# Loads and row squares of a streaming encoder layer: an early function table, third-group weight blocks in more places, squares tied behind another tile

## The chip, the cores and the metric

The kernel runs on one core of one Trainium2 chip. The metric is device time in microseconds of one execution. Before the change the median of three runs is 2246.33 us (2240.46 to 2246.46). One more execution was recorded by the hardware profiler; its own time is 2244.01 us.

Engines are named as in the profile: PE multiplies matrices (PEld loads its weights), DVE and ACT work on vectors, POOL is the general-purpose engine, SP issues most DMAs. Each engine runs its own instructions in order and waits on semaphores for the others.

## The reference

One layer over 2048 prompt rows and 64 rows of a running stream, all float32, width 1024. Only what the change touches is shown; what follows (output projection, squared-ReLU MLP of width 4096, final norm) is left out.

```python
def _rmsnorm(x, gain):
    y = xf * lax.rsqrt(jnp.mean(xf * xf, axis=-1, keepdims=True) + EPS)
    return (y * gain).astype(x.dtype)
...
a  = _rmsnorm(hp, norm1[l])
z  = a @ w_in                       # columns: qa, ka, va | qr, kr, vr, gr
qa, ka, qr, kr = rotated by position
attn_o = _swa_prompt(qa, ka, va, sinks[l])     # window of three 64-row chunks
ret_o, s_p = _retention_prompt(qr, kr, vr)     # decayed state per head
r = ret_o * lax.rsqrt(mean(ret_o * ret_o) + EPS) * silu(gr)
hp = hp + concat([attn_o, r]) @ w_out
hp = hp + _sqrelu_mlp(_rmsnorm(hp, norm2[l]), w_up, w_down)
```

The first norm's factor per row, rsqrt(mean(x²)+EPS), is not multiplied into x. It is applied to the projection's result, so it is first needed when a row tile's projection is rotated.

## The kernel before

The program has four stages: projection with attention and retention (to about 720 us), output projection, MLP up, MLP down. Every float32 product is made of three products of rounded parts: an operand is split into a high part (ACT copies it to the float32r type) and a low part (DVE or POOL subtracts); PE multiplies high·high, high·low and low·high (lines 548, 549, 551).

The first stage runs in two phases (`ph`), each with half of the heads. In a phase the weight columns stand in three groups `ci` = 0, 1, 2 (384, 512, 512 columns), each of eight blocks of 128 rows. `load_w` (113) brings a block into a raw buffer, `weights` (129) splits it: `split_scaled` writes the high part on ACT (86) and the low part on DVE (87). The rows of x come in 17 tiles: sixteen of 128 prompt rows (0 to 15) and one of 64 stream rows, tile 16, called S here. A tile passes through `group` (535) once per column group: 24 products on PE (16 for S, whose two parts share the array). Phase 0 begins with the pair (S, 0): groups (S,0), (0,0), (S,1), (0,1), (S,2), (0,2), written here as (tile, group); then come tiles 1 to 13 one by one, and the pair (14, 15).

After a tile's groups come its attention steps (`att_a` to `att_e`) and retention steps (`ret_a` to `ret_e`). `att_a` scales and rotates the first group (234, and 203 to 206: three DVE products and one POOL add into `zr`), `ret_a` rotates the second into `qk`, `ret_v` takes the third: two scaled copies (356) and the tanh of the gate (361). The transposes for attention (254, 217, 218) go to PSUM; ACT copies them into `qT` (256) and `kw` (222), which the scores `s` (286, 287) need. The transposes of `qk` go to `ptr` (369).

`load_aux` (164) brings a tile's rows by token into `xk` (one buffer) and its rotation table into `rt` (two buffers). In phase 0 it also makes the row factors: ACT squares `xk` and sums (172), then five short POOL instructions make `rs`, `hrs`, `ss` and `rsv` (174 to 179). `load_x` (143) brings the tile's transposed rows into `xr` (one buffer); ACT copies the high part (160), POOL subtracts the low part (161).

What sets the order: PE and SP follow the order in which the code is written (`manual_schedule`, 572); when a step of attention or retention comes due between PE's products is decided by a table of costs and delays (496, 497). ACT, DVE and POOL are ordered by a scheduler that estimates times. SP waits in order: a load into a buffer that is not free holds back all loads behind it, and it keeps eight DMAs under way. Loads on SP and copies that prepare later weights (625, DRAM to DRAM, with additions issued by POOL at 622) use the same DMA engines.

Buffers that matter here: `raw` has three (116), so the fourth block of a group loaded that way waits until the first is split. `wraw` (115) uses eight places of the pool `qp`, which hold the split blocks of other groups later. `ph` and `pl` (320, 321) are two buffers each, first used by `att_d`.

```python
    ws[0, 1] = weights(0, 1, [load_w(0, 1, k, True) for k in range(NK)])
    ...
    ws[0, 2] = weights(0, 2)
```

## Time and profile before

| | |
|---|---|
| median of 3 runs | 2246.33 us |
| profiled execution, its own time | 2244.01 us |
| its span (first to last instruction) | 2242.2 us |
| PE busy | 2210.4 us (99%) |
| DVE, ACT, POOL busy | 1468.0, 1117.6, 441.5 us |
| clock granted to PE, mean over the span | 0.992 of full |
| DMA moved | 515.91 MB, mean 230 GB/s |

How to read it: PE is busy nearly throughout, so time can leave the run only where PE stands still or runs at the lower of its two clocks (1.2 instead of 2.4 GHz). The list of waits names both, by the instruction that waited and the one that ended the wait; windows of the span give busy time and granted clock of each stretch. Ends of matrix products are modelled in the profile, so a distance between two starts is surer than a duration.

### The profile page before, as it was taken

How to read it: one execution, taken by the hardware profiler on the slowest of the kernel's cores; microseconds unless marked ns; L12 is line 12 of the kernel's file. 1: busy time of each engine (PE TensorE's matmuls, PEld its weight loads, DVE VectorE, ACT ScalarE, POOL GpSimd, SP SyncE). 2: the span in 40 equal slices, each digit the busy share in tenths (PEclk: the TensorE clock that was granted, in tenths of full speed). 3: DMA queues.
4: the chain of work that ended last, by engine and by line, in shares of the span. 5: the costliest groups of instructions: out<-in, count | busy, mean ns of one | idle time of the engine just before them, and what ended most of it. 6: DMA issues, size and time to landing. Idle time of an engine off the chain costs nothing.

```text
span 2242.2 us, 35648 instructions
## 1 busy us (share of the span) xinstructions
PE 2210.4 (99%) x13274; PEld 2114.8 (94%) x13274; DVE 1468.0 (65%) x2461; ACT 1117.6 (50%) x1982; POOL 441.5 (20%) x547
## 2 busy tenths in 40 slices
PE   8999999999999999999999999999999999999998
PEld 6888878888888899999999999999999999999998
DVE  5565446555556567787688668667666876677664
ACT  5454445444434443456565657556554444554452
POOL 4544443444433222200000000000001100120011
PEclk9999999999999999999999999999999999999999
DMA  6557864588644689579699769776976787677662
GB/s 193 162 170 188 224 175 143 145 206 216 159 107 122 208 289 337 186 265 361 229 319 353 268 230 323 235 233 210 367 259 228 266 288 240 229 277 268 236 209 80
DMA packets 240877, 515.91 MB, mean 230 GB/s; under 512 B 20144, under 2 KB 126320, under 8 KB 236608
## 3 DMA queue, kind: packets, MB, share of 16 engines
q1 hardware_dynamic: 231616, 469.62, 61.7%
q0 software_dynamic: 8512, 43.29, 9.3%
q8 instruction: 104, 1.70, 0.3%
q10 hardware_dynamic: 576, 0.72, 0.1%
q14 instruction: 69, 0.57, 0.1%
HBM read 411.19 MB, written 169.54 MB: 259 GB/s over the span
## 4 chain that ended last, share of the span: by engine, by line
PE 93%; DMA 3%; DVE 1%; POOL 1%; ACT 1%; issue 1%; SPq 0%; DVEq 0%; POOLq 0%; ACTq 0%
PE y L1073 10%; PE y L1074 9%; PE y L1072 9%; PE z L548 7%; PE z L549 7%; PE z L551 6%; PE b L901 4%; PE b L902 4%; PE b L900 4%; PE y L763 3%; PE y L765 3%; PE y L764 3%; PE a L901 3%; PE c L901 3%; PE a L902 3%; PE c L902 3%
## 5 line engine op out<-in xcount | busy, mean ns | idle before, releaser
L1073 PE MATMUL y<-vl,wd 128*128 128x352 f32 x1344 | 436.4, 325 | 0.0
L1074 PE MATMUL y<-vh,wd 128*128 128x352 f32 x1344 | 434.7, 323 | 0.0
L1072 PE MATMUL y<-vh,wd 128*128 128x352 f32 x1344 | 433.0, 322 | 0.0
L548 PE MATMUL z<-w,xh 128*128 128x512 f32 (+1 forms) x816 | 327.2, 401 | 0.7 <-DVE xh L161 0.6
L549 PE MATMUL z<-w,xh 128*128 128x512 f32 (+1 forms) x816 | 310.5, 380 | 4.8 <-DVE w L87 4.8
L1022 POOL TENSOR_TENSOR acc<-acc,sq 128x352 f32<-128x352 f32 x41 | 70.2, 1712 | 1216.5 <-ACT sq L1018 1216.5
L484 ACT ACTIVATE wd<-dr 128x1024 fp32r<-128x1024 f32 x168 | 177.4, 1056 | 252.6 <-PE y L1074 171.8
L484 ACT ACTIVATE wu<-upr 128x512 fp32r<-128x512 f32 x336 | 209.4, 627 | 179.3 <-PE b L902 88.8
L551 PE MATMUL z<-w,xl 128*128 128x512 f32 (+1 forms) x768 | 289.5, 377 | 0.1
L485 DVE TENSOR_TENSOR wu<-upr,wu 128x512 fp32r<-128x512 f32 x336 | 231.0, 693 | 71.0 <-ACT wu L484 56.4
L485 DVE TENSOR_TENSOR wd<-dr,wd 128x1024 fp32r<-128x1024 f32 x168 | 209.2, 1247 | 102.1 <-ACT wd L484 96.8
L1072 PEld LDWEIGHTS y<-vh,wd 128*128 128x128 f32 x1344 | 253.9, 189 | 0.0
L1074 PEld LDWEIGHTS y<-vh,wd 128*128 128x128 f32 x1344 | 252.4, 188 | 0.0
L1073 PEld LDWEIGHTS y<-vl,wd 128*128 128x128 f32 x1344 | 252.0, 188 | 0.0
L901 PE MATMUL b<-al,wu 128*128 128x352 f32 x576 | 185.8, 323 | 0.0
L900 PE MATMUL b<-ah,wu 128*128 128x352 f32 x576 | 185.6, 322 | 0.0
L902 PE MATMUL b<-ah,wu 128*128 128x352 f32 x576 | 185.4, 323 | 0.0
L549 PEld LDWEIGHTS z<-w,xh 128*128 128x128 f32 x816 | 156.8, 192 | 26.3 <-DVE w L87 8.3
L548 PEld LDWEIGHTS z<-w,xh 128*128 128x128 f32 x816 | 156.5, 192 | 19.7 <-DVE xh L161 0.8
L551 PEld LDWEIGHTS z<-w,xl 128*128 128x128 f32 x768 | 145.1, 189 | 23.8 <-DVE xl L161 0.4
L485 DVE TENSOR_TENSOR vl<-rv,vh 128x1408 fp32r<-128x1408 f32 x84 | 138.1, 1647 | 38.8 <-ACT vh L484 38.4
L484 ACT ACTIVATE vh<-rv 128x1408 fp32r<-128x1408 f32 x84 | 116.0, 1380 | 59.8 <-DMA rv<-vscr 42.2
(286 smaller groups left out, 4737.7 us busy)
## 6 DMA issues: line engine op xcount, KB each, us to landing
rv<-vscr SPq DMA_DIRECT2D x84, 704.0 KB, 5.4
vscr<-C SPq DMA_DIRECT2D x48, 1056.0 KB, 5.7
upr<-uscr SPq DMA_DIRECT2D x192, 256.0 KB, 4.7
dr<-sscr SPq DMA_DIRECT2D x96, 512.0 KB, 4.6
upr<-in_wup SPq DMA_DIRECT2D x144, 256.0 KB, 3.6
dr<-in_wdn SPq DMA_DIRECT2D x72, 512.0 KB, 5.2
uscr<-in_wup POOLq DMA_DIRECT2D x16, 1024.0 KB, 10.2
sscr<-in_wdn POOLq DMA_DIRECT2D x16, 1024.0 KB, 9.3
```

Source lines behind the costliest of these rows:

```text
L484: nc.scalar.activation(h, x, AF.Copy)
L485: nc.vector.tensor_sub(l, x, h.bitcast(F32))
L548: nc.tensor.matmul(z[:, :n], xh[:, k], wh, start=k == 0, stop=False)
L549: nc.tensor.matmul(z[:, :n], xh[:, k], wl, start=False, stop=k == NK - 1 and xl is None)
L551: nc.tensor.matmul(z[:, :n], xl[:, k], wh, start=False, stop=k == NK - 1)
L900: nc.tensor.matmul(o, wh, ah[:, k], start=k == 0 and i in (1, 6, 5), stop=False, skip_group_check=True)
L901: nc.tensor.matmul(o, wh, al[:, k], start=False, stop=False, skip_group_check=True)
L902: nc.tensor.matmul(o, wl, ah[:, k], start=False, stop=k == 3 and i in (2, 4, 3), skip_group_check=True)
L1022: nc.gpsimd.tensor_add(self.acc, self.acc, sq)
L1072: nc.tensor.matmul(o, wh, vh, start=f == 0, stop=False)
L1073: nc.tensor.matmul(o, wh, vl, start=False, stop=False)
L1074: nc.tensor.matmul(o, wl, vh, start=False, stop=f == 15)
```

## The change

Three things are changed.

1. A tiny ACT copy (`first`) stands at the start. ACT loads its function table in front of its first activation; the table load was part of the first weight block's split, which waits for that block's DMA.
2. The loads at the start are put in another order. Of column group 1, four blocks are loaded ahead of S's `xk` and `rt` instead of behind them. Of group 2, three blocks go to `raw`, four to the `ph` and `pl` buffers and all seven are issued ahead of the cache, state and aux loads; the eighth goes to `raw` behind the aux load of tile 0.
3. The square of a tile's rows with its POOL steps becomes a function of its own, `token_norm`. It is called later than the load: for the two first tiles at the start, else at the beginning of the tile's own first group (or of the group 0 of the tile before, where the load has been issued by then), and it is tied (`issue_after`) behind the last tanh (361, `ret_v`) or the last high-part copy of `att_a` (239) that was written before it.

```diff
+    first = cp.tile([128, 3], F32, name="first")
+    nc.scalar.activation(first, mhalf, AF.Copy)
...
-    def load_w(ph, c, k, spare=False):
+    def load_w(ph, c, k, spare=False, tag=None):
...
+            wk.tile([128, 512], F32, name="waraw", tag=tag, bufs=2) if tag else \
...
             nc.sync.dma_start(xk[:T], xtok[t0:t0 + T])
+            squares[t] = xk
         nc.sync.dma_start(rt[:T], rot[t0:t0 + T])
-        if ph == 0:
+        return rt
+
+    squares = {}
+    last_act = [None]
+
+    def token_norm(t):
+        t0, T = tok(t)
+        xk = squares.pop(t)
+        with tc.issue_after(last_act[0].ins) if last_act[0] is not None else ExitStack():
             nc.scalar.activation(xk[:T], xk[:T], AF.Square, accum_out=ss[:T, t:t + 1])
...
-        nc.scalar.activation(hl[:T, 768:832], zr[:T, 5], AF.Copy)
+        last_act[0] = nc.scalar.activation(hl[:T, 768:832], zr[:T, 5], AF.Copy)
...
-        nc.scalar.activation(sig[:T], gz, AF.Tanh, scale=hrs[:T, t:t + 1])
+        last_act[0] = nc.scalar.activation(sig[:T], gz, AF.Tanh, scale=hrs[:T, t:t + 1])
...
-    nc.sync.dma_start(rd, rdec)
...
+    raws = [load_w(0, 1, k, True) for k in range(4)]
+    nc.sync.dma_start(rd, rdec)
     xs[a] = [*x0, load_aux(*a)]
-    ws[0, 1] = weights(0, 1, [load_w(0, 1, k, True) for k in range(NK)])
+    raws += [load_w(0, 1, k, True) for k in range(4, NK)]
+    ws[0, 1] = weights(0, 1, raws)
+    token_norm(a[1])
+
+    raws = [load_w(0, 2, k, tag=(None, None, None, "ph", "ph", "pl", "pl")[k]) for k in range(NK - 1)]
     caches[0] = load_cache(0)
+    xs[b] = [*x1, load_aux(*b)]
+    token_norm(b[1])
+    raws.append(load_w(0, 2, NK - 1))
     load_states(0)
-    xs[b] = [*x1, load_aux(*b)]
     nc.sync.dma_start(sk, sinks)
     nc.gpsimd.tensor_scalar(nsk, sk, -1.0, None, op0=ALU.mult)
-    ws[0, 2] = weights(0, 2)
+    ws[0, 2] = weights(0, 2, raws)
...
+        for u in [u for u in squares if (0, u) in tiles[:n_ + 2] and ci == 0 or (0, u) == tiles[n_]]:
+            token_norm(u)
```

The change moves instructions in three places. SP at the start, behind the last block of group 1 (`raw` and `waraw` are blocks of group 2, `cf` the cache, `xk` and `rt` of tile 0; the numbers are those of the buffers). Before:

```order
L117 DMA wraw_211<-in_w1 128x512
L431 DMA cf_237<-in_cv 128x64
L432 DMA cf_237<-in_ck 128x64
L455 DMA sts0_240<-in_sret 128x128
L455 DMA sts1_242<-in_sret 128x128
L169 DMA xk_245<-in_xtok 128x1024
L170 DMA rt_244<-in_rot 128x384
L601 DMA sk_77<-in_sinks 128x8
L117 DMA raw_257<-in_w1 128x512
L117 DMA raw_262<-in_w1 128x512
L117 DMA raw_267<-in_w1 128x512
L117 DMA raw_272<-in_w1 128x512
```

The same place now:

```order
L120 DMA raw_239<-in_w1 128x512
L120 DMA raw_241<-in_w1 128x512
L120 DMA raw_243<-in_w1 128x512
L120 DMA waraw_245<-in_w1 128x512
L120 DMA waraw_247<-in_w1 128x512
L120 DMA waraw_249<-in_w1 128x512
L120 DMA waraw_251<-in_w1 128x512
L442 DMA cf_253<-in_cv 128x64
L443 DMA cf_253<-in_ck 128x64
L172 DMA xk_257<-in_xtok 128x1024
L174 DMA rt_256<-in_rot 128x384
L120 DMA raw_267<-in_w1 128x512
```

Seven blocks of group 2 moved ahead of seven other loads; one stands behind `xk` and `rt`.

POOL at the start, from the add that makes `zr` of tile S to the adds that make `qk` of S and of tile 0; `ms`, `rs`, `ss`, `hrs`, `rsv` are row factors of tile 0, the `cf` loads belong to phase 1. Before:

```order
L206 TENSOR_TENSOR zr<-rot_327,rot_328 64x320
L245 DMA out<-zr 64x64
L602 TENSOR_SCALAR nsk<-sk 128x8
L174 TENSOR_SCALAR ms<-ss 128x1
L431 DMA cf<-in_cv 128x64
L432 DMA cf<-in_ck 128x64
L175 TENSOR_TENSOR rs<-ms,mhalf 128x1
L177 TENSOR_SCALAR ss<-ms 128x1
L176 TENSOR_SCALAR hrs<-rs 128x1
L178 TENSOR_SCALAR rsv<-rd,rs 128x4
L206 TENSOR_TENSOR zr<-rot_391,rot_392 128x320
L206 TENSOR_TENSOR qk<-rot_423,rot_424 64x512
```

Now:

```order
L217 TENSOR_TENSOR zr<-rot_329,rot_330 64x320
L256 DMA out<-zr 64x64
L186 TENSOR_SCALAR ms<-ss 128x1
L187 TENSOR_TENSOR rs<-ms,mhalf 128x1
L189 TENSOR_SCALAR ss<-ms 128x1
L442 DMA cf<-in_cv 128x64
L443 DMA cf<-in_ck 128x64
L620 TENSOR_SCALAR nsk<-sk 128x8
L188 TENSOR_SCALAR hrs<-rs 128x1
L190 TENSOR_SCALAR rsv<-rd,rs 128x4
L217 TENSOR_TENSOR zr<-rot_386,rot_387 128x320
L217 TENSOR_TENSOR qk<-rot_418,rot_419 64x512
```

`nsk` and the two `cf` issues moved behind the power that makes `rs`; what stands ahead of `qk` is the same set.

ACT in the middle of phase 0, one tile's period, from its tanh (`sig`) to the copies `qT` and `kw`; `xk` with its number shows which tile's rows are squared. Before (tile names differ by the numbers alone):

```order
L361 ACTIVATE sig_3025<-z_2955,hrs_83 128x256
L322 ACTIVATE ph_3051<-pt_3046 128x512
L322 ACTIVATE ph_3060<-pt_3055 128x512
L400 ACTIVATE ro_3077,s2_3075<-pr_3067 128x128 x2
L234 ACTIVATE zr_3104<-z_3034,rs_82 128x64
L335 ACTIVATE ob_3138<-po_3133 64x512
L238 ACTIVATE hl_3112<-zr_3104 128x6x64
L239 ACTIVATE hl_3112<-zr_3104 128x64
L426 ACTIVATE mr_3153<-prt_3150 128x256
L172 ACTIVATE xk_3357,ss_81<-xk_3357 128x1024
L256 ACTIVATE qT_3173<-pq_3168 128x4x2x64
L222 ACTIVATE kw_2865<-pk_3175 128x2x128
```

Now:

```order
L372 ACTIVATE sig_3020<-z_2950,hrs_85 128x256
L184 ACTIVATE xk_2883,ss_83<-xk_2883 128x1024
L333 ACTIVATE ph_3053<-pt_3048 128x512
L333 ACTIVATE ph_3062<-pt_3057 128x512
L411 ACTIVATE ro_3079,s2_3077<-pr_3069 128x128 x2
L245 ACTIVATE zr_3106<-z_3036,rs_84 128x64
L346 ACTIVATE ob_3133<-po_3128 64x512
L249 ACTIVATE hl_3114<-zr_3106 128x6x64
L250 ACTIVATE hl_3114<-zr_3106 128x64
L437 ACTIVATE mr_3148<-prt_3145 128x256
L267 ACTIVATE qT_3168<-pq_3163 128x4x2x64
L233 ACTIVATE kw_2867<-pk_3170 128x2x128
```

The square left its place in front of `qT` and stands behind the tanh. It is also another tile's: before, the rows squared after `zr` of tile u are those of tile u+2; now those of tile u itself are squared just ahead of its `zr`.

## Rows read from the trace of the kernel before

**Rows 1.** The first line of the page.

```profile
span 2242.2 us, 35648 instructions
```

**Rows 2.** The list of waits, PE alone, whole span: waiting instruction, what it waited for, total us, times, longest.

```profile
PE s L286 <- ACT kw L222: 8.1, 4, 4.6
PE z L549 <- DVE w L87: 4.8, 7, 1.5
```

**Rows 3.** Windows of the span at the start: stretch, its length, then busy us and instructions of PE, PEld, DVE, ACT, POOL, the granted clock, DMA share, GB/s.

```profile
20.00:24.00 4.00, 4.00 (x11) 2.87 (x12) 3.28 (x6) 1.37 (x3) 4.00 (x1) 0.57 0.96 332
...
36.00:40.00 4.00, 3.01 (x12) 1.93 (x11) 3.08 (x6) 1.39 (x2) 2.85 (x1) 0.68 0.67 188
40.00:44.00 4.00, 4.00 (x12) 3.11 (x12) 1.94 (x8) 2.47 (x8) 0.20 (x1) 0.50 0.76 263
```

**Rows 4.** The timeline of the first 25 us: start, duration, engine, line and operation, out<-in, in brackets the idle time before it and what ended it.

```profile
3.77 1.28 ACT L86 ACT_TABLE_LOAD   x1 [3.77 <-DMA wraw<-in_w]
...
8.06 2.20 ACT L86 ACTIVATE w<-wraw,gsb 128x384 fp32r<-128x384 f32 x4 [0.25 <-DMA wraw<-in_w]
...
14.41 1.06 ACT L172 ACTIVATE xk<-xk 64x1024 f32<-64x1024 f32 x1 [0.82 <-DMA xk<-in_xtok]
...
16.24 0.49 PE L548 MATMUL z<-w,xh 128*128 128x512 f32 x1
...
18.05 0.54 DVE L203 SCALAR_TENSOR_TENSOR rot<-zz,rs,rt 64x320 f32<-64x320 f32 x1
...
19.10 4.05 DVE L87 SCALAR_TENSOR_TENSOR w<-wraw,gsb,w 128x512 fp32r<-128x512 f32 x6
19.26 4.75 POOL L206 TENSOR_TENSOR zr<-rot,rot 64x320 f32<-64x320 f32 x1
19.89 0.50 PE L549 MATMUL z<-w,xh 128*128 128x512 f32 x1 [0.98 <-DVE w L87]
...
24.21 0.40 PE L548 MATMUL z<-w,xh 128*128 128x512 f32 x1
...
24.44 0.40 PE L549 MATMUL z<-w,xh 128*128 128x512 f32 x1
```

**Rows 5.** The view of one tile, `wraw` (the raw blocks of groups 0 and 1): durations in ns (min/median/max), first and last start, and the time from a load's issue to its landing.

```profile
L86 ACT ACTIVATE w<-wraw,gsb x16: 598/662/713, 5.1 to 20.5; 128x384 fp32r<-128x384 f32 x8, 128x512 fp32r<-128x512 f32 x8
...
DMA to landing us min/median/max: 2.5/4.5/6.1
```

**Rows 6.** The timeline around the third column group, columns as in rows 4.

```profile
24.91 1.04 ACT L172 ACTIVATE xk<-xk 128x1024 f32<-128x1024 f32 x1
...
26.68 0.61 POOL L431 DMA_DIRECT2D cf<-in_cv  x1 [0.36 <-issue]
...
27.85 1.17 POOL L175 TENSOR_TENSOR rs<-ms,mhalf 128x1 f32<-128x1 f32 x1
...
30.62 1.30 POOL L206 TENSOR_TENSOR zr<-rot,rot 128x320 f32<-128x320 f32 x1 [0.71 <-DVE rot L205]
30.64 0.49 PE L548 MATMUL z<-w,xh 128*128 128x512 f32 x1
...
32.68 2.24 POOL L206 TENSOR_TENSOR qk<-rot,rot 64x512 f32<-64x512 f32 x1 [0.75 <-DVE rot L205]
...
33.32 0.49 PE L549 MATMUL z<-w,xh 128*128 128x512 f32 x1 [0.79 <-DVE w L87]
...
38.10 0.80 PE L549 MATMUL z<-w,xh 128*128 128x512 f32 x1 [0.28 <-DVE w L87]
...
40.25 0.79 PE L548 MATMUL z<-w,xh 128*128 128x512 f32 x1
...
40.84 0.63 PE L549 MATMUL z<-w,xh 128*128 128x512 f32 x1
```

**Rows 7.** The chain of work that ended last, between 206 and 288 us: start, duration, what.

```profile
206.11 8.60 DMA xk<-in_xtok
214.73 1.15 ACT xk L172 x2
...
274.09 11.22 DMA xk<-in_xtok
...
287.29 0.53 PE s L286
```

**Rows 8.** Windows of the span around the last of these places, columns as in rows 3.

```profile
285.00:289.00 4.00, 1.72 (x8) 1.72 (x9) 0.93 (x2) 1.91 (x4) 2.19 (x6) 0.70 0.92 276
289.00:296.00 7.00, 7.00 (x26) 5.59 (x26) 2.40 (x11) 2.20 (x10) 1.64 (x3) 0.68 0.83 172
```

**Rows 9.** The timeline of the tile after it, columns as in rows 4; SPq is SP issuing a DMA.

```profile
297.86 0.47 ACT L361 ACTIVATE sig<-z,hrs 128x256 f32<-128x256 f32 x1
...
299.95 0.59 SPq L149 DMA_DIRECT2D xr<-in_xt  x1
...
301.94 0.59 SPq L169 DMA_DIRECT2D xk<-in_xtok  x1
...
303.51 0.31 ACT L234 ACTIVATE zr<-z,rs 128x64 f32<-128x64 f32 x1 [2.48 <-PE z L551]
...
317.45 1.06 ACT L160 ACTIVATE xh<-xr 128x1024 fp32r<-128x1024 f32 x1 [1.01 <-PE z L549]
...
318.92 0.47 ACT L361 ACTIVATE sig<-z,hrs 128x256 f32<-128x256 f32 x1
```

More of the change, by code (lines that the diff above doesn't have):

```diff
@@ L179, in load_aux @@
                                     op0=ALU.mult)
-        return rt
     def xprep(n):
```

## Prediction

> **What bounds the kernel now.** I read the page's first part, the list of PE's waits, windows of the granted clock, and then the timeline and the chain of waits where PE stands. PE is busy for 99% of a span of 2242.2 us [rows 1]. So only two kinds of time can go: PE standing still, and PE at 1.2 GHz. In the list of waits [rows 2] two entries bear on the change: PE's scores `s` wait for ACT's copy `kw`, 8.1 us in 4 waits, and the first products wait for DVE's split of a weight block, 4.8 us in 7. The windows show the second kind: the granted clock is 0.57 from 20 to 24 us, 0.68 from 36 to 40, 0.50 from 40 to 44 [rows 3], and about 0.7 from 285 to 296 [rows 8]. Each such stretch follows waits of PE.
>
> The profiled execution took 2244.01 us, 1.8 more than its span; the sum is made against it. It lies 2.3 us under the median of the three runs, within their spread of 6 us.
>
> **Losses at the start.** Where nothing disturbs it, PE starts products of 512 columns 0.23 us apart (24.21, 24.44) [rows 4]. Group (S,1), 16 products, should take 3.7 us and takes 8.0, from 16.24 to 24.21 [rows 4]: 4.3 lost, to waits for DVE (0.98 before the product at 19.89 is the longest) and to the low clock. Group (S,2) should need 3.5 us from its first start to its last and takes 7.5, from 30.64 to 38.10 [rows 6]: 4.0 lost. The blocks of group 2 go through three raw buffers, and each wait is for a block that was loaded late. Then (0,2), from 40.25, runs its first 4 us at the low clock (a product shows 0.63 us instead of 0.40) [rows 4, 6]: 2.0 lost. Together 10.3 us.
>
> **Losses in the middle.** The chain of waits [rows 7] shows the mechanism. SP issues `xk` at 206.11 behind two copies; it lands 8.60 us later; ACT, in order, waits for it with the square, and `qT` and `kw` stand behind the square; PE's `s` starts only then. It comes four times, the last with a landing of 11.22 us, after which `s` starts at 287.29. The four waits are the 8.1 us [rows 2]. The low clock behind the last is 4 x 0.30 + 7 x 0.32 = 3.4 us of full-speed time [rows 8]. It began near 286.6 (1.2/0.5 = 2.4 us of the first window), so 0.7 us of it fell into the wait and cost nothing: 3.1 us. Together 11.2.
>
> **The change part by part.**
>
> Function table. The load takes 1.28 us at 3.77, when the first block has landed [rows 4]. Early, it lies in idle time of ACT. But from 8.06 ACT already waits for landings with the blocks behind it (0.25) [rows 4], and the second tile's rows come after those. So only the first two blocks run earlier. I take 0.2 us; bounds 0 (all of it hidden by landings) and 1.3 (all of it on the path).
>
> Order of the loads of group 1. Four blocks pass `xk` and `rt` of S, and ACT no longer waits 0.82 us for `xk` before its first block [rows 4]. The last block still has the same bytes in front of it, and lands no earlier: its ACT part starts at 20.5 now [rows 5], and a block takes 0.66 there. DVE adds about 0.7 per block (six in 4.05) [rows 4], and the three products of S's rotation (18.05 to 19.10) now stand in front of the last three blocks. That puts the last block at about 22.7 and the group's end at 23.0 to 23.7 instead of 24.21. I take 0.5. Bounds: -1.2 (the 3.4 us at low clock in 20 to 24 [rows 3] are followed by a second such stretch, 1.7, less the 0.5) and +2.0 (the low clock, 1.5, does not come either).
>
> Group 2. The seven loads follow group 1 without a wait for a buffer. ACT needs 7 x 0.66 us from about 21.2, DVE some 5.5 us from 22.7: all are split at 28.5 to 30.5, before (S,2) begins. Its 4.0 us of waits go. What is late next is POOL: the square of tile 0 (24.91 before [rows 6]) stands behind seven blocks and six small copies on ACT, about 28; then come the power, 1.17 us, two DMA issues of 0.61, four short steps, the add for `zr` of tile 0, 1.30, and the one for `qk` of S, 2.24 [rows 6]. Counted from 29.2 with 0.2 to 0.3 for a short step and 1.2 for the rotation, `qk` is there at 36.0, and its transposes let (0,2) begin at 36.7 instead of 40.25. That is 3.5 us, 0.7 of which the two edits before have taken: 2.8 for this one. PE waits some 1 to 2 us in front of the transposes. Behind so short a wait I expect most of the 2.0 us of low clock in (0,2) to go and take 1.5. Bounds of both: 0.3 (one more POOL add as long as the 4.75 us at 19.26 [rows 4], and the low clock stays) and 6.5 (no wait for `qk` at all).
>
> Squares. Of each tile the square (1.06 us and a read) and five POOL steps are moved, not added. They no longer stand in front of `qT` and `kw`, and `xk` is then long there: SP issues it nearly a tile's period, 21 us (the tanhs at 297.86 and 318.92 [rows 9]), before it is used, against landings of 8.60 to 11.22 [rows 7]. That takes away the four waits, 8.1, and the low clock, 3.1. Price of the new place: the square comes behind the tanh, and `ph`, the sums `ro` and, by way of `rs`, `zr` queue behind it. From the tanh at 297.86 to `zr` at 303.51 there are 5.65 us [rows 9]; the tanh, the square and its read take 1.7, two short POOL steps and the power 1.5 at most, so `rs` is ready 2 us early. `ph` comes 1.25 us later and has more than that before it is used. Cost 0; lower bound of the part 8.1 (the low clock returns), upper 12.
>
> Sum: 0.2 + 0.5 + 2.8 + 1.5 + 8.1 + 3.1 = 16.2 us; 2244.0 - 16.2 = 2227.8, so 2228 us.
>
> **A rule against it.** The add for `zr` of S takes 4.75 us for 64x320 elements beside six DVE splits in a row, while twice as many rows took 1.30 at 30.62 [rows 4, 6]. The Trainium skill, "SBUF — State Buffer", section "SBUF: two separate sides", says that a DVE operation with two SBUF inputs and a POOL operation that reads SBUF take a shared port pair in turn, each for its whole instruction. The split is such an operation, so by that rule the change, which puts fifteen splits nearly back to back, would hold up POOL just where `qk` waits for it. The trace agrees as far as the 4.75 goes.
>
> **The rivals.**
> (a) POOL takes over at the start. If each of the two adds before the transposes takes 4.75 us, 3.45 and 2.5 more, (0,2) begins after 40.25 and the start gives about nothing, the missing low clock against the longer wait: 2244.0 - 11.2 = 2232.8. For it: the 4.75. Against: it needs every add to meet splits, and by 31 us they are through. 0.12. The skill's rule above is this rival's mechanism.
> (b) Only the start gains: the square is still an ACT instruction in front of PSUM copies, and the wait for `kw` becomes one for `ph`. 2244.0 - 5.0 = 2239.0. For: it sits in front of `ph` in every tile. Against: its operand has landed by then. 0.10.
> (c) Slower: SP loses its lead. `xk` has one buffer, and SP waits in order. Today the next `xk` goes out at 301.94 [rows 9], as its square is over early; now it must wait for the square behind the tanh, and the copies and `xr` behind it gather there. `xr`, issued at 299.95 and needed at 317.45, has 17.5 us [rows 9]; issued 2 to 3 us later and behind 2 MB more (three copies and `xk`, 0.5 MB each), it lands within 12 us by the slowest landing of rows 7. It decides from a landing of about 15 us on. Then PE waits for rows in the six tiles with dense traffic, an estimated 2.5 us (the rest of a landing of 18) and 1.7 of low clock (half of the 3.4 us above) each, 25 us: 2244.0 - 16.2 + 25 = 2253. 0.08.
> (d) Neither half does what it says: the start bound by landings, the middle by copies ahead of `kw`. 2244. 0.04.
>
> **How the numbers follow.** The forecast, 2228, has 0.66; its own range is 2223 to 2235 (20.5 to 9.1 gained: start 8.5 to 1.0, middle 12 to 8.1). Two runs of this kernel can be told apart from about 0.3%, 6.7 us, so faster means under 2239.6. Faster: the forecast, (a) and half of (b), 0.83; same: half of (b), (d) and a little of (c), 0.10; slower 0.07. The range for 8 in 10 reaches from 2220, where a later wait of PE goes as well, to 2241, which takes in (a) and (b).
>
> **What would show it.** Right: in the list of PE's waits `s` for `kw` is gone, the wait for DVE's weights is under 3 us, and a wait of 1 to 2 us for `qk` or `ptr` stands near 35 us; (0,2) begins near 36.7; the clock is 1.00 from 285 to 296, shifted by some 15 us; the square follows the tanh without a wait for DMA. Wrong: ACT waits for `xk` behind the tanh, or PE's products for `xh` or `xl` in tiles 6 to 13 (c); a POOL add over 4 us between 30 and 38 us (a); a new PE wait of over 0.3 us in each tile (b).

## The result and the profile after

The kernel after takes 2221.48 us, median of 4 runs (2218.57 to 2223.31), against 2244.83 us for the kernel before in 4 runs; the ratio is 0.9894, 95% interval 0.9882 to 0.9907. That is 23.4 us less, where the prediction had 16.2 less and 2228; the time lies 1.5 us under the forecast's own range, 2223 to 2235, and inside the one for 8 in 10, 2220 to 2241. The steps did not all come out, and one part of the gain stands in none of them.

The page of the kernel after, first line, as [rows 1]:

```profile
span 2219.7 us, 35656 instructions
```

The list of waits of the kernel after, PE alone, whole span, as [rows 2]:

```profile
PE pss L391 <- ACT rkT L385: 3.6, 1, 3.6
...
PE ptr L380 <- POOL qk L217: 1.3, 1, 1.3
...
PE z L559 <- ACT w L88: 1.1, 1, 1.1
...
PE z L560 <- DVE w L89: 1.1, 3, 0.5
```

The four waits of `s` for `kw`, 8.1 us in [rows 2], are gone. The wait for DVE's weights has fallen from 4.8 to 1.1 us, and the foreseen wait for `qk` is there with 1.3 us. What heads the list now is `pss` waiting for `rkT`; the kernel before had that wait too.

Windows of the kernel after, columns as in [rows 3]: the first four stretches answer to [rows 3], the next two to [rows 8] (that work now comes some 15 us earlier), the last lies in the last stage.

```profile
20.00:24.00 4.00, 2.75 (x6) 1.49 (x7) 3.55 (x7) 4.00 (x8) 3.75 (x5) 0.65 1.05 386
24.00:28.00 4.00, 4.00 (x11) 3.12 (x10) 4.00 (x7) 3.53 (x7) 4.00 (x2) 0.50 1.00 326
36.00:40.00 4.00, 2.71 (x17) 2.19 (x16) 4.00 (x8) 1.49 (x3) 2.70 (x2) 1.00 0.15 49
40.00:44.00 4.00, 4.00 (x21) 3.06 (x20) 2.81 (x9) 2.97 (x11) 2.55 (x2) 1.00 0.00 0
270.00:274.00 4.00, 4.00 (x27) 3.44 (x26) 1.29 (x3) 0.87 (x2) 0.41 (x1) 1.00 1.06 301
274.00:281.00 7.00, 7.00 (x40) 6.05 (x39) 4.23 (x14) 3.89 (x14) 2.93 (x4) 1.00 1.04 241
1800.00:2000.00 200.00, 200.00 (x1252) 200.00 (x1251) 140.34 (x146) 99.78 (x100) 25.97 (x14) 1.00 0.76 260
```

In the middle the clock is 1.00 where it was 0.70 and 0.68. From 40 us on it is 1.00 where it was 0.50. But from 20 to 28 us PE now has eight microseconds at little more than half speed; of before the first four are in [rows 3], with 0.57.

The timeline of the start, columns as in [rows 4]:

```profile
0.74 1.28 ACT L69 ACT_TABLE_LOAD   x1 [0.74 <-PEq L1210]
...
18.66 1.06 ACT L184 ACTIVATE xk<-xk 64x1024 f32<-64x1024 f32 x1 [0.65 <-DMA xk<-in_xtok]
...
20.47 0.50 PE L559 MATMUL z<-w,xh 128*128 128x512 f32 x1 [1.12 <-ACT w L88]
...
22.01 5.58 POOL L190 TENSOR_SCALAR rsv<-rd,rs 64x4 f32<-64x4 f32 x1
...
22.17 2.06 DVE L89 SCALAR_TENSOR_TENSOR w<-wraw,gsb,w 128x512 fp32r<-128x512 f32 x3
...
26.81 0.68 DVE L568 TENSOR_TENSOR zz<-z,zb 64x512 f32<-64x512 f32 x1
...
34.83 0.30 POOL L190 TENSOR_SCALAR rsv<-rd,rs 128x4 f32<-128x4 f32 x1
...
36.70 1.26 POOL L217 TENSOR_TENSOR qk<-rot,rot 64x512 f32<-64x512 f32 x1 [0.76 <-DVE rot L216]
...
38.02 0.46 PE L380 MATMUL ptr<-idf,qk 64*128 64x64 f32 x4 [1.29 <-POOL qk L217]
...
38.41 0.50 PE L559 MATMUL z<-w,xh 128*128 128x512 f32 x1
```

Group (0,2) begins at 38.41 instead of 40.25; the forecast was 36.7. (These three times, here and in the prediction, are those of the first product behind the transposes. In the order of the code it still belongs to the eighth block of (S,2); the first product of (0,2) itself comes two products later, at 41.27 before and 38.97 now.) POOL needs 5.58 us for 64 x 4 elements of `rsv`, and 0.30 us for twice as many rows later.

ACT in an undisturbed tile of the kernel after, as in [rows 9], and what SP waits for between 44 and 740 us:

```profile
280.76 0.47 ACT L372 ACTIVATE sig<-z,hrs 128x256 f32<-128x256 f32 x1
281.12 1.07 ACT L184 ACTIVATE xk<-xk 128x1024 f32<-128x1024 f32 x1
```

```profile
SPq L172 <- ACT xk L184: 209.0, 12, 19.5
```

The square follows the tanh with no idle time in front of it. SP does stand for it, 209 us in 12 waits, as rival (c) had it; PE waits for none of what is queued behind.

**Where the 22.4 us of the two traces lie.** PE runs the same 13274 products in both kernels, in the same order but for four near 765 us, so the n-th product of one trace can be set against the n-th of the other, and the distance from each product to the next can be compared. Differences of more than 50 ns are waits and low clock; the smaller ones, thousands of them, show how closely products follow each other when nothing waits. Summed by stretch of the kernel before (us, negative is a gain):

```
stretch (us)     over 50 ns   up to 50 ns
0-45                -3.5          -0.3
45-206               0.0          -1.0
206-294            -12.0          -0.4
294-380             -0.1          -0.6
380-700             +0.6          -1.7
700-770             -0.1          -0.3
770-1590             0.0          -0.1
1590-2242           +0.2          -3.4
```

The columns add up to -14.9 and, before rounding, -7.6. The start gave 3.5 of the 5.0 predicted, the middle 12.0 of 11.2. The third part, 7.6 us, is no wait and no clock: in 200 us of the last stage PE ran 1252 products, and 1243 before.

### The profile page after: what moved, and what is told of

It reads as the page before. It is cut to its first block, busy times and chain, and to the rows that moved or that the text cites. A ratio compares the mean times of both kernels' runs of the same rounds, so it can differ in the third digit from the quotient of the medians.

```text
span 2219.7 us, 35656 instructions
## 1 busy us (share of the span) xinstructions
PE 2196.7 (99%) x13274; PEld 2108.1 (95%) x13274; DVE 1466.4 (66%) x2461; ACT 1115.6 (50%) x1983; POOL 444.8 (20%) x547
## 4 chain that ended last, share of the span: by engine, by line
PE 95%; DMA 2%; DVE 1%; issue 1%; ACT 1%; SPq 0%; POOL 0%; DVEq 0%; ACTq 0%; POOLq 0%
PE y L1094 9%; PE y L1093 9%; PE y L1092 9%; PE z L559 7%; PE z L560 7%; PE z L562 7%; PE b L922 4%; PE b L921 4%; PE b L920 4%; PE y L783 3%; PE y L785 3%; PE y L784 3%; PE a L922 3%; PE a L921 3%; PE a L920 3%; PE c L922 3%
```

## The experiments

### Control, and the two halves apart

`c_before` and `c_after` are the two kernels unchanged. `e_start` is the kernel after with this edit; the scheduler then puts the squares where they stood before, so that only the start differs from the kernel before:

```
 def token_norm(t):
     ...
-    with tc.issue_after(last_act[0].ins) if last_act[0] is not None else ExitStack():
+    with ExitStack():
```

`e_squares` is the kernel before with `token_norm` and its tie, which is the kernel after with the function table and the loads put back (the diff is against the kernel after, and leaves out the loads of group 1):

```
-    first = cp.tile([128, 3], F32, name="first")
-    nc.scalar.activation(first, mhalf, AF.Copy)
...
-    raws = [load_w(0, 2, k, tag=(None, None, None, "ph", "ph", "pl", "pl")[k]) for k in range(NK - 1)]
...
-    ws[0, 2] = weights(0, 2, raws)
+    ws[0, 2] = weights(0, 2)
```

> The kernel before, unchanged, as a control with a profile of its own. In the two traces at hand the kernel after is 22.4 us ahead at its last product: 3.5 by 44 us, 12 to 13 between 210 and 294 us, and the other 6 or so grow slowly where nothing waits (in the last stage the products come 161.1 to 162 ns apart before and 160.0 after). Theory A: that slow part is how one execution differs from the next and has nothing to do with the change. Then this profile shows its own distance, anywhere from 160.0 to 161.2 ns, and the ratio to the kernel before is 1.000 within 0.001. Theory B: it belongs to the kernel before. Then its last stage shows 161 ns or more again, and the kernel after 160.0 again.

> The kernel after, unchanged, on the same chip as the control. Theory A (slow part is no part of the change): against the control's profile the same places show up, 3.5 us by 44 us and 12 to 13 us between 210 and 294, and the sum of places is 16 to 17 us, ratio 0.9925 to 0.993. Theory B (it belongs to the change): 22 to 23 us, ratio 0.9895 to 0.990, with 160.0 ns between products of the last stage against 161 or more in the control.

> The kernel after with one thing taken back: the squares are not tied, and then the scheduler leaves them on ACT in front of qT and kw, as before. So only the start (function table and order of loads) is changed. Theory A (two halves that add up): 3.5 us ahead of the control by 44 us, and the four waits of s for kw are there again, 6 to 9 us in all; 2241 us on a control of 2244.8, ratio 0.998 to 0.999. Rival: the waits in the middle came from where the transfers of the start pushed the later ones, so that they go with the start alone; then 12 to 17 us, ratio 0.993.

> The kernel before with the squares tied behind the tanh as after, and the start (function table, order of loads) as before. Theory A: nothing gained by 44 us, 11 to 13 us between 210 and 294 us, the waits of s for kw gone; 2232.5 us on a control of 2244.8, ratio 0.994 to 0.995. Rival: the middle needs the start too; then one or more waits of s for kw stay, and less than 6 us are gained, ratio above 0.997. With theory B on the slow part it would gain up to 6 us more than A says.

Measured against the kernel before on the same chip: `c_before` 2244.94 us, ratio 0.9991 (0.9982 to 1.0001); `c_after` 2222.14, 0.9900 (0.9881 to 0.9919); `e_start` 2237.13, 0.9960 (0.9946 to 0.9974); `e_squares` 2232.32, 0.9943 (0.9929 to 0.9957). The halves add up: 0.40% and 0.57% against 1.00%.

PE's waits in `e_start`, then in `e_squares`:

```profile
PE s L297 <- ACT kw L233: 11.8, 3, 7.3
...
PE ptr L380 <- POOL qk L217: 2.7, 1, 2.7
```

```profile
PE z L558 <- DVE w L87: 5.8, 6, 1.5
PE pss L389 <- ACT rkT L383: 3.3, 1, 3.3
```

With the old place of the square the waits for `kw` are back; with the tie alone they are gone, whatever the start. In the stretch from 206 to 294 us `e_squares` gains 12.9 us on the control, `c_after` 12.9 as well. So the middle is settled: the place of the square alone does it.

The start alone gave 9 us by the medians (0.40% of 2245; its profiled execution, the slowest of six, gained 2.5), and only 2.6 of them lie over 50 ns in the first 45 us. Against the control the steps under 50 ns come to -7.8 us in `c_after`, and the rows below show with which kernels they go: the last stage of the control, and of `e_start`.

```profile
1800.00:2000.00 200.00, 200.00 (x1243) 200.00 (x1242) 141.67 (x151) 94.36 (x96) 22.51 (x12) 1.00 0.74 252
```

```profile
1800.00:2000.00 200.00, 200.00 (x1252) 200.00 (x1251) 142.33 (x152) 96.24 (x98) 23.72 (x13) 1.00 0.76 255
```

`e_squares` has 1243 there, `c_after` 1252. Two profiles of one kernel agree to 0.1 us in this sum, so theory A, that it is a difference between executions, has fallen; something in the start does it, 1900 us later.

The start itself is not so steady. The control, the same program as in [rows 3], has no low clock at all in their first window:

```profile
20.00:24.00 4.00, 4.00 (x15) 2.16 (x14) 2.93 (x6) 1.31 (x4) 3.69 (x2) 1.00 0.93 330
```

And `c_after` has the granted clock 0.57 from 40 to 44 us, behind a wait for `qk` of 2.7 us, where the first profile of the same kernel shows 1.00 behind 1.3 us. So the change gives 3.5 us in the first 45 by the one pair of profiles and 0.9 by the other. More profiles narrow it: the product that stands at 60.15 us in the kernel before comes at 59.9 to 61.5 in six profiles with the start of the kernel before (two of that kernel, and the four of the next section), and at 56.3 to 58.6 in four with the start of the change (the two of the kernel after, `e_start` and `e_notable`). That is 3.0 us on average, where 5.0 were predicted.

### An unused tile of 32 or 64 bytes

The copy that brings the function table in has a tile of its own, which moves what is allocated behind it by 32 bytes per partition; the pools that are filled from the other end of the memory (`xp`, `wB`, `wd`) stay. Among what moves are the buffers from which PE streams the weight blocks of groups 1 and 2, and later `ah`, `al`, `vh` and `vl`. `e_pad32` and `e_pad64` are the kernel before with a tile that nothing uses; every instruction is as before (in `e_pad64` there is 16 for the 8):

```
     nc.gpsimd.memset(mhalf, -0.5)
+    pad = cp.tile([128, 8], F32, name="pad")
```

`e_less32` and `e_less64` move the other way, with `nsk`, and in `e_less64` `sk` too, put behind the buffers:

```
-    nsk = cp.tile([128, 2, 4], F32, name="nsk")
...
     rd = k1.tile([128, 2, 4], F32, name="rd")
+    nsk = k1.tile([128, 2, 4], F32, name="nsk")
```

> The kernel before plus one tile of 32 bytes per partition that nothing uses; the instructions of all engines stay the same, only the addresses of what is allocated behind it move by 32 bytes. In the traces so far PE's products come a little closer together, without any wait, in each of the two kernels that bring the function table in first, and not in the two that don't: 160.0 ns against 161.1 in the last stage from about 1740 us on, 233.8 against 235.6 for the first product of a triple in the first stage; summed over the steps under 50 ns it is 7.6 to 7.8 us. Theory A (the new tile of that copy moves the addresses, and PE reads some of them faster): 160.0 ns here, 7.6 us faster than the control, ratio 0.9966. Theory B (the instruction, or the other order of loads, does it): 161.1 ns, ratio 1.000.

> The same with a tile of 64 bytes. Theory A1 (what counts is the address within 64 bytes): as the kernel before, 161.1 ns in the last stage, ratio 1.000. Theory A2 (any other address would do): 160.0 ns, ratio 0.9966. Theory B: 161.1 ns, ratio 1.000, here and with 32 bytes.

> The kernel before with the small tile nsk moved behind the block of eight operand buffers, so that these buffers and what lies around them start 32 bytes lower and the working tiles of the first stage stay where they were; all instructions stay the same. So far: buffers at 18816 (0 over a multiple of 128) 160.0 ns, then 161.1 ns between products of the last stage; at 18848 (32 over) 160.0 throughout, 7.6 us less; at 18880 (64 over) 162 to 163.4 ns, 19 us more. Theory M128 (the place within 128 bytes decides): 18784 is 96 over, not seen yet, no forecast for it except that it may be any of these. Theory D (each step upward of the buffers changes it because of what they share a stretch of memory with, so that a step down is no mirror of a step up): likewise open; what tells is the pair with the next run. Theory W (the working tiles of the first stage, which moved as well in the earlier runs, matter and not these buffers): as before, 161.1 ns, ratio 1.000.

> The same with sk and nsk moved, so that the eight buffers start at 18752, 64 bytes lower and 64 over a multiple of 128. Theory M128: as with 64 bytes more, 162 to 163.4 ns in the last stage and 10 us lost in the stage before it, 19 us slower than the control, ratio 1.009. Theory M64 has fallen already (64 more was not as 0). Theory D: something else, such as the 160.0 or 161.1 ns seen before. Theory W: as before, ratio 1.000.

Measured; the second column is where the allocator puts the first buffer, in bytes over a multiple of 128, the third the products in the window from 1800 to 2000 us, the fourth the sum of steps up to 50 ns against the control (us), the last the ratio to the kernel before on the same chip:

```
kernel     start       products   small steps   median us   ratio (95%)
before     18816: 0      1243          0         2244.83    1
e_pad32    18848: 32     1252         -7.5       2236.16    0.9968 (0.9955 to 0.9980)
e_pad64    18880: 64     1227        +20.6       2266.76    1.0093 (1.0078 to 1.0107)
e_less32   18784: 96     1243         +3.3       2244.65    0.9995 (0.9983 to 1.0007)
e_less64   18752: 64     1227        +21.8       2268.02    1.0110 (1.0096 to 1.0125)
```

The last stage of `e_pad32`, and of `e_pad64`:

```profile
1800.00:2000.00 200.00, 200.00 (x1252) 200.00 (x1251) 140.18 (x148) 96.14 (x97) 23.81 (x13) 1.00 0.75 256
```

```profile
1800.00:2000.00 200.00, 200.00 (x1227) 200.00 (x1226) 139.82 (x149) 95.09 (x96) 18.65 (x11) 1.00 0.73 243
```

In all of them PE is busy for the whole 200 us at clock 1.00; only the count of products tells them apart. 32 bytes that hold nothing give the 7.5 us: theory A, with an effect as large as the tile's in the change. Neither theory on 64 bytes was right: 64 more is not as before, and not as 32 more, but 20 us slower. 64 less is slow in the same way, which is what theory M128 asked for: the two addresses are 128 apart and both 64 over a multiple of 128. Theory W has fallen with it, since the working tiles of the first stage stay where they were there. The 3.3 us in the small steps of `e_less32` do not show in its time, the median of 12 runs; the interval ends 1.6 us above the kernel before. Which operand of PE it is can be told for the last stage: the allocator leaves the weight tiles `wd` at the same addresses in all five kernels and moves `vh` and `vl`, which PE streams. Why PE is slower there, no run tells; nor why the kernel before changes from 160.0 to 161.1 ns between products near 1748 us, right behind two products of a norm in the middle of a step.

### The function table, and the order of the loads of group 1

`e_notable` is the kernel after without the copy, its tile kept. `e_g1old` is the kernel after with the loads of group 1 in the old order:

```
     first = cp.tile([128, 3], F32, name="first")
-    nc.scalar.activation(first, mhalf, AF.Copy)
```

```
-    raws = [load_w(0, 1, k, True) for k in range(4)]
     nc.sync.dma_start(rd, rdec)
     xs[a] = [*x0, load_aux(*a)]
-    raws += [load_w(0, 1, k, True) for k in range(4, NK)]
+    raws = [load_w(0, 1, k, True) for k in range(NK)]
```

> The kernel after without the first copy, so that the function table is loaded when the first block has landed, as before; the copy's tile stays, so that no address moves. By the prediction's step the table is worth 0.2 us (bounds 0 and 1.3): against the kernel after the first product of the first block is late by 0.8 us and that is back by about 12 us. Time 2222 to 2222.7, ratio to the kernel before 0.990 to 0.9905. Theory A on the spacing: 160.0 ns as after. Theory B1 (the instruction does it): 161.1 ns and 7.6 us slower than after, 2229.7.

> The kernel after with the first four blocks of the second column group back behind the token rows and rotation of the short tile, as before; the rest of the start stays. Theory A (this reordering cost, since the last block of that group landed at 21.5 us instead of 20.1 and products waited at the low clock): the group's end comes 1 to 2 us earlier than in the kernel after, POOL's chain to qk of the short tile starts earlier, and the time is 1 to 2.5 us shorter, 2220 to 2221. Rival, the prediction's step: the reordering gains 0.5 us, and taking it back gives 2222.5 to 2223.

`e_notable`: 2219.74 us, ratio 0.9890 (0.9875 to 0.9906), and within 0.2 us of `c_after` in the first 45 us of the trace. Fetching the table early is worth nothing that can be measured. `e_g1old`: 2216.56 us, ratio 0.9879 (0.9865 to 0.9892), the lowest median of this study. Its interval overlaps those of `c_after` and `e_notable`, so the times alone do not show a gain. The traces do: in the first 45 us that of `e_g1old` gains 4.6 us over `c_after` and 2.4 over the first profile of the kernel after, and the first product behind the transposes comes at 35.56 to 36.67 in the three kernels with the old order (`e_g1old`, and `e_dveadd` and `e_rkt` below), at 37.42 to 38.99 in the four profiles with the new one. So this part of the change is a loss. The windows of `e_g1old` at the start:

```profile
20.00:24.00 4.00, 4.00 (x13) 2.05 (x14) 4.00 (x7) 3.93 (x7) 4.00 (x1) 1.00 1.08 381
24.00:28.00 4.00, 4.00 (x19) 3.32 (x18) 4.00 (x7) 3.75 (x10) 3.10 (x2) 1.00 0.85 280
```

The clock stays at 1.00, where the kernel after has 0.65 and 0.50. But that is not what the order costs: `e_start` and `e_notable`, with the new order, have 1.00 in both windows too, and `e_dveadd`, with the old one, has 0.71 and 0.87. The tile `wraw` in the kernel after, then in `e_g1old`, as [rows 5]:

```profile
L88 ACT ACTIVATE w<-wraw,gsb x16: 600/662/725, 3.8 to 21.8; 128x384 fp32r<-128x384 f32 x8, 128x512 fp32r<-128x512 f32 x8
...
DMA to landing us min/median/max: 2.5/4.3/7.4
```

```profile
L88 ACT ACTIVATE w<-wraw,gsb x16: 596/663/712, 4.0 to 20.5; 128x384 fp32r<-128x384 f32 x8, 128x512 fp32r<-128x512 f32 x8
...
DMA to landing us min/median/max: 2.7/4.4/5.5
```

The last block of group 1 starts on ACT at 21.8 instead of 20.5 (also 20.5 in [rows 5]), and a block takes up to 7.4 us to land instead of 6.1 or 5.5. This too is not steady: over all profiles that block starts at 20.4 to 21.8 with the new order and at 20.1 to 21.1 with the old, and `e_start`, with 20.4, is late all the same. What the four with the new order share is the square of S. It waits for `xk`, which now has four blocks in front of it, and starts at 17.3 to 18.7 us (18.66 in the timeline above) instead of 14.0 to 15.0. From there to the square of tile 0, ACT in the kernel after, then in `e_g1old`:

```profile
29.25 0.53 ACT L249 ACTIVATE hl<-zr 64x384 fp32r<-64x384 f32 x1 [1.17 <-POOL zr L217]
...
30.13 1.04 ACT L184 ACTIVATE xk<-xk 128x1024 f32<-128x1024 f32 x1
```

```profile
14.41 1.06 ACT L184 ACTIVATE xk<-xk 64x1024 f32<-64x1024 f32 x1 [0.73 <-DMA xk<-in_xtok]
...
26.57 0.53 ACT L249 ACTIVATE hl<-zr 64x384 fp32r<-64x384 f32 x1 [0.25 <-POOL zr L217]
...
27.45 1.05 ACT L184 ACTIVATE xk<-xk 128x1024 f32<-128x1024 f32 x1
```

With a late square of S, POOL's row factors of S fall beside DVE's row of splits, where `rsv` takes 5.1 to 5.6 us (next section). The addition for `zr` of S comes behind it, and ACT is idle for it 1.2 to 2.1 us (0.25 or less with the old order). The square of tile 0, on which POOL's way to `qk` hangs, starts at 29.1 to 30.2 instead of 27.1 to 28.8. PE's wait for `qk` is 1.3 us in the first profile of the kernel after, but 2.5 to 2.7 in the other three with the new order, and in these the clock falls behind it: 0.57 from 40 to 44 us in `c_after`, 0.69 and 0.88 in the two windows from 36 to 44 us in `e_start`, 0.62 and 0.52 in `e_notable`. That the order causes the loss is shown by `e_g1old`; the chain is read from the traces, and no run takes one link out of it.

### POOL beside the splits

In `e_g1old` the product `rsv` is quick, and the addition for `zr` of S is what takes long (its POOL timeline):

```profile
17.33 0.30 POOL L190 TENSOR_SCALAR rsv<-rd,rs 64x4 f32<-64x4 f32 x1
...
19.27 7.28 POOL L217 TENSOR_TENSOR zr<-rot,rot 64x320 f32<-64x320 f32 x1
```

The same addition takes 4.75 us in [rows 4] and 0.90 in the kernel after, where it begins at 28.33. In the kernel after, POOL's `rsv` ends at 27.59, just after DVE's `zz` (26.81 to 27.49 in the timeline above), which reads PSUM and comes between the splits; in `e_g1old` the addition ends at 26.55, and `zz` runs from 25.73 to 26.41. So in these two the hold follows the place and not the instruction: what POOL begins in the long row of splits stays until DVE turns to an operation on PSUM. (In [rows 4] DVE's row ends without one, and the addition ends 0.7 us after it.) In a shorter row POOL does get its turn. In `e_start` the addition stands beside the three splits behind `zz`:

```profile
26.43 1.73 POOL L217 TENSOR_TENSOR zr<-rot,rot 64x320 f32<-64x320 f32 x1
```

```profile
26.04 2.68 DVE L89 SCALAR_TENSOR_TENSOR w<-waraw,gsb,w 128x512 fp32r<-128x512 f32 x3
```

It ends at 28.16, before the splits do, and the three of them take 2.68 us, 2.08 in `e_g1old`, where POOL has nothing to do beside the last two. What decides when POOL gets its turn is open. That a split holds up POOL is what the Trainium skill says in "SBUF — State Buffer", section "SBUF: two separate sides", with one difference: by that rule the port pair is taken for one whole instruction at a time, and here POOL does not get its turn between one split and the next, seven of them in the kernel after.

`e_dveadd` is `e_g1old` with that addition on DVE:

```
-        last_pool[0] = nc.gpsimd.tensor_add(dst, t1, t2)
+        if (T, nb) == (64, 5) and last_pool[0] is None:
+            nc.vector.tensor_add(dst, t1, t2)
+        else:
+            last_pool[0] = nc.gpsimd.tensor_add(dst, t1, t2)
```

> The kernel after with the old order of the loads of group 1 (the fastest so far, 2216.6 us), and with the addition for zr of the short tile on DVE instead of POOL. In that fastest kernel POOL's addition takes 7.28 us, from 19.27 to 26.55, while DVE's splits run without a gap; in the kernel after, the tiny product rsv (64 x 4 elements) takes 5.58 us beside such splits and 0.30 elsewhere. Theory P (POOL is held as long as the splits follow each other, and what hangs on it sets qk of the short tile): without that addition no POOL instruction before 35 us takes over 2 us, hl of the short tile and the square of tile 0 come 0.3 to 1 us earlier, PE's wait for qk (1.7 us) falls to about 1, and the time by 0.5 to 1 us, 2215.5 to 2216. Rival Q (ACT's own row of splits sets that square, POOL's hold is hidden behind it): the wait stays within 0.3 us of 1.7, the time within 0.5 us of 2216.6. If another POOL instruction beside the splits now takes several us, the hold follows the place and not the instruction.

Measured: 2219.63 us, ratio 0.9891 (0.9878 to 0.9904), no gain on `e_g1old`. Its PE waits and a row of its DVE timeline:

```profile
PE ptr L383 <- POOL qk L220: 0.9, 1, 0.9
```

```profile
20.97 0.48 DVE L218 TENSOR_TENSOR zr<-rot,rot 64x320 f32<-64x320 f32 x1
```

On DVE the addition takes 0.48 us, no POOL instruction is long any more, and the wait for `qk` falls from 1.7 to 0.9 us. But `qk` of S does not come earlier. POOL's addition for it in `e_g1old`, then in `e_dveadd`:

```profile
34.36 1.26 POOL L217 TENSOR_TENSOR qk<-rot,rot 64x512 f32<-64x512 f32 x1 [0.76 <-DVE rot L216]
```

```profile
34.96 1.26 POOL L220 TENSOR_TENSOR qk<-rot,rot 64x512 f32<-64x512 f32 x1 [0.77 <-DVE rot L216]
```

The wait is shorter because PE reaches it later: the addition stands in DVE's row, group 1 ends later and runs at the low clock (by PE's products the kernel is 1.4 us behind `e_g1old` at 23.6 us, and 0.6 at 36). ACT's copy `hl` of S follows ACT's own splits without a wait, where in `e_g1old` it waited 0.25 us for POOL. So with the old order the hold is hidden behind ACT's row, which is rival Q's mechanism, though its time (within 0.5 us of 2216.6) did not come either. The profile of `e_dveadd` is 5.9 us longer than that of `e_g1old`; 0.7 lie in the first 45 us, 1.7 near 366 and 2.7 from 713 to 738 us, a stretch in which the two profiles of the kernel after differ by 3.0 as well.

### The longest wait that is left

> The fastest kernel so far (after, with the old order of the loads of group 1, 2216.6 us), in which the longest wait of PE that is left, pss for ACT's copy rkT (3.6 us at 361.7, with the low clock behind it), is taken on: for the two tiles at the change of phase that copy is made by DVE, right behind rqT, instead of by ACT, which stands in its row for raw blocks and rows that have yet to land. Theory A (the same pattern as with the squares: an engine in order waits for a transfer with an instruction that PE needs standing behind it): rqT is done at 363.0 and the copy at 363.5, PE's wait falls to under 2 us, and the nine products at half speed behind it (0.32 us instead of 0.17, 1.4 us in all) mostly go: 2.5 to 4 us faster, 2212.6 to 2214, ratio to the kernel before 0.986 to 0.987. Rival B (DVE stands behind ACT's parts of the same blocks, so that its copy comes no earlier, or the next product waits for the split rows xh instead): the wait stays over 3 us or another of the same size takes its place, within 1 us of 2216.6.

```
+        if c.ph == 0 and c.t in (S - 2, S - 1):
+            nc.vector.tensor_copy(c.rkT[:, :, :T], pv[:, 2:4])
+        else:
             nc.scalar.activation(c.rkT[:, :, :T], pv[:, 2:4], AF.Copy)
```

Measured: 2217.23 us, ratio 0.9870 (0.9848 to 0.9892): not to be told from `e_g1old`. PE's waits:

```profile
PE y L785 <- ACT wo L498: 1.5, 1, 1.5
...
PE z L565 <- POOL xl L164: 1.2, 1, 1.2
...
PE y L1096 <- DVE wd L499: 1.0, 1, 1.0
...
PE pss L394 <- DVE rkT L386: 0.3, 1, 0.3
```

The wait for `rkT` fell from 3.6 to 0.3 us, and by PE's products the kernel is 5.0 us ahead of `e_g1old` right behind it (363.8 us; 0.5 of them from before 45 us). Then it gives back 1.2 us to POOL's `xl` of the next tile, 0.9 near 381 us, some 3.4 from 700 to 770 us and 1.3 near 1570 us, and ends 2.0 us behind. Theory A was right on the place, rival B on the time (within 1 us of 2216.6). Whether the later losses follow from the edit was not tested.

## Why the prediction was right, and where it was not

**What bounds the kernel.** The prediction said that only two kinds of time can go, PE standing still and PE at 1.2 GHz. This is the step that failed most. There is a third, which the list of waits and the granted clock do not show: how closely products follow each other at full clock. It gave 7.6 of the 22.4 us and came by a side effect of the new tile, 32 bytes of address. The count of products in a window shows it.

**Function table.** Forecast 0.2, bounds 0 and 1.3; measured nothing (`e_notable`). Its instruction was the right thing to price low, its tile was not priced.

**Order of the loads of group 1.** Forecast a gain of 0.5, bounds a loss of 1.2 and a gain of 2.0; measured a loss of 2.4 to 4.6 us (`e_g1old`), outside the bounds. The step that failed is "Four blocks pass `xk` and `rt` of S": only ACT's gain by it was priced, and what hangs on `xk` of S was put at nothing. Its square starts some 3.5 us later, POOL's row factors fall beside the splits, `zr` of S makes ACT wait 1.2 to 2.1 us, and the square of tile 0, put at about 28, starts at 29.1 to 30.2 (27.45 in `e_g1old`). That the last block's ACT part starts at 20.5 was wrong in two of four profiles (21.8 and 21.5), but right or nearly so in the others (20.4 and 20.9), which lose as well. Why it is late in the two was not tried.

**Group 2.** Forecast 2.8 and 1.5 for the low clock; with group 1 in the old order the start gains 5.5 to 5.8 us on the kernel before, of which the table has nothing. The mechanism was right: the waits for the splits go, POOL's `qk` is late next. With the old order PE waits 0.9 to 1.7 us for it, the clock stays at 1.00 from 36 to 44 us, and (0,2) begins at 36.06 in `e_g1old`, with the forecast at 36.7. In the order of the change it begins at 37.4 to 39.0, and the forecast wait of 1 to 2 us, with little low clock behind it, came in one profile of four. One count was off: the 4.0 us lost in (S,2) assume that all its 16 products start by 38.10, and only 14 do, so 4.4 are lost there.

**Squares.** Forecast 8.1 and 3.1 us; measured 12.0 between 206 and 294 us, 12.9 in `e_squares` with nothing else changed. Right in mechanism, place and size; the new place costs nothing, as priced.

**Rivals.** (a) came to pass in part: POOL was held as the rule says, but it held a product of 256 elements, before 30 us, and what it cost on the path is ACT's wait of 1.2 to 2.1 us for what came behind. (c) did too: SP waits for the square 209 us in all, and its price is none, since what it issues still lands in time. (b) and (d) have fallen with `e_squares` and `e_start`.

**The number.** 16.2 was 5.0 for the start and 11.2 for the middle. In the trace it is 3.5 and 12.0, and 7.6 that was not in the sum, less about 0.7 elsewhere. So the total was nearer than its parts: without the tile's 32 bytes the kernel after would have come out near 2229, an estimate (2221.5 and 7.6). The tile alone takes the time under 2223. That the wider range still holds it is luck, since its fast end, 2220, stood for a later wait of PE. And the range's other end does not follow from its parts: their lower bounds for the start (0, -1.2 and 0.3) add up to a loss of 0.9, where the range has a gain of 1.0.

## What to carry to other kernels

Where an engine works in order, ask of each instruction that waits for a transfer what is queued behind it; tying it behind work that is later anyway took away four waits of PE and the low clock behind the last. A change that allocates anything moves the operands behind it: compare the count of products in a quiet window before crediting its instructions, and try a pad of 32 bytes. When a load passes another, ask as well what hangs on the one that is passed. Test each reordering of loads alone, since one part here was a loss that the others hid: the change without it takes 2216.56 us, against 2219.7 to 2222.1 with it, and only the traces of the start show that difference clearly.

## What the runs showed of the hardware that was not expected

PE's rate at full clock depends on where its operands lie (in the last stage, the streamed one): 1252, 1243 and 1227 products in 200 us of the same instructions, 29 us between the fastest and the slowest place over the whole kernel (-7.5 and +21.8), with buffers 128 bytes apart equally slow. POOL can be kept out for 5 to 7 us by DVE operations that follow each other every 0.66 us. And the low clock is no fixed price of a wait: of two profiles of the kernel before, one has it from 20 to 24 us and the other not.
